# Seven block products instead of eight in one feed-forward layer, and low parts made by adding DMAs

## The chip, the cores and the metric

The kernel runs on one core of one Trainium2 chip. The metric is the device time of one execution in microseconds (us). Two runs of the kernel before took 2017.01 and 2012.07 us, median 2014.54 us. Engines are named as the profile names them: PE (matmuls), PEld (its weight loads), DVE, ACT, POOL, SP (which issues the loads).

## The reference

Two layers of a diffusion backbone. A latent stream and a context stream of 256 tokens each, 1024 features wide, go through the same weights: a gated feed-forward part (FFN), token mixing (differential attention and a Fourier branch, merged by gates), and a second FFN. In the last layer the context stream stops after it has given keys and values. What matters here is the FFN:

```python
def swiglu(u, w_in, w_out):
    a, b = jnp.split(u @ w_in, 2, axis=-1)
    return (jax.nn.silu(a) * b) @ w_out

def ffn_sublayer(x, m, i, g, w_in, w_out):
    u = modulate(rms_norm(x, g), m, i)
    return x + 0.5 * m[:, 3 * i + 2][:, None] * swiglu(u, w_in, w_out)
```

`w_in` is 1024 x 5632: a half for `a` and a half for `b`. All numbers are 32-bit floats.

## The kernel before

**Layout.** Features lie on the 128 partitions, tokens along the free axis: columns 0 to 255 are the latent tokens (LAT), 256 to 511 the context tokens (CTX). `u` is eight chunks of 128 features (KC = 8).

**High and low parts.** A float32 operand is split into `hi`, the value rounded to the matmul's own format, and `lo`, what is left. A product is three matmuls (`mm3`, L373 to L375): hi x hi, hi x lo, lo x hi. In the second FFN of the last layer, with 256 columns, `mm_wide` (L380, L381) puts the two that share `hi` into one matmul of 512 columns.

**The stream of weights.** All weights pass, in order of use, through one stream of 392 blocks of 128 x 1024 numbers (512 KB), eight 128 x 128 tiles each. `Stream.next` asks SP to load blocks some way ahead (`ahead[0]`) and splits blocks a shorter way ahead (`ahead[1]`). The split (`split_pieces`, L192 and L193) is a copy on ACT that rounds (`whi`), and a subtraction raw - hi (`wlo`) on DVE or POOL; the string `lo_on` says which by the block's number ("vvp": two on DVE, one on POOL). Layer 1's FFNs also compute the modulation values, one block of `w_mod` per weight block (`tick`): a dot product on DVE per stream (`junk`, L302), and a small operation on POOL (`mval`, L315 and L317).

**Buffers.** One pool of 46 slots of 4 KB per partition (tag "s") holds raw blocks, hi and lo, `u`, and the FFN's gated values `g` (22 slots of hi and lo side by side). PSUM has 8 banks of 512 numbers.

**The FFN** (`ffn`). 22 pairs j, each of two blocks: `pa` gets 128 features of `a`, `pb` of `b`. Two pairs come first, k by k, each stream by itself, while the norm's results arrive. From the third pair on: eight tiles into `pa`, eight into `pb`, each tile an `mm3` of 512 columns, 48 matmuls a pair; then `gated` (L625 to L627) and `low` (L631). `project_out` multiplies the 22 g's by `w_out`, 66 tiles per three blocks, adds the residual on DVE (L462), and sums squares for the next norm on POOL (`acc`, L424).

**The order of the work** is written out by hand: each engine executes its instructions in the order in which the Python code issues them, and waits on semaphores where the code's reads and writes demand it. A DMA is issued by the engine whose queue it stands in and waits there for its source and its buffer.

## Time and profile before

| | us |
|---|---|
| median of two runs | 2014.54 |
| the profiled execution's own time | 2016.41 |
| its span, first to last instruction | 2014.5 |
| PE busy | 1992.3 |
| DVE busy | 1211.7 |
| ACT busy | 823.0 |
| POOL busy | 735.6 |

Stages by the PE's instructions in the trace, us from the span's start: layer 1's first FFN to 396, mixing and its output to 816, second FFN to 1178; layer 2's first FFN from 1178 (pairs three to five from 1202.6, the sixth pair from 1235.2, the output from 1420.2 to 1541), mixing to 1815, second FFN from 1815 (input from 1828, output from 1942.4), end at 2014.5. The granted clock of the core was 0.997 of full. Where a row of windows is shown, its columns are: the stretch, its length, the busy time and number of instructions (in brackets) of PE, PEld, DVE, ACT and POOL, the granted clock, the share of the 16 DMA engines, GB/s. A matmul's own duration in the trace overlaps the next one's, so its price is taken from the distance of starts, or from a window divided by its count.

### The profile page before, as it was taken

The numbers are of one execution on the slowest core, as the hardware profiler recorded it, in microseconds if no ns is written. First come the engines' busy times: TensorE is split into PE (matmuls) and PEld (weight loads), VectorE is DVE, ScalarE is ACT, GpSimd is POOL, SyncE is SP. The second block draws the span as 40 slices with busy tenths as digits, with TensorE's granted clock in tenths as the row PEclk, the third lists the DMA queues.
The fourth block names the chain that finished last, engine by engine and source line by source line (L and its number), as shares of the span: only waits on it lengthen the run. The fifth ranks groups of instructions, "written<-read, shape, count | busy, mean of one in ns | idle before, by whom it ended". The sixth has DMA issues, their size and how long they took to land.

```text
span 2014.5 us, 26969 instructions
## 1 busy us (share of the span) xinstructions
PE 1992.3 (99%) x10388; PEld 1702.2 (84%) x10388; DVE 1211.7 (60%) x1832; ACT 823.0 (41%) x1335; POOL 735.6 (37%) x492
## 2 busy tenths in 40 slices
PE   8999999999999999999999999999999999999998
PEld 7888888888888888988888898888888889898887
DVE  5877786667777334677777252332324687776652
ACT  3432232256666323523223242222323565666661
POOL 0334455546553013243358410111222454224463
PEclk9999999999999999999999999999999999999999
DMA  9555565413222334455569332222421333555461
GB/s 378 204 169 176 167 210 210 165 58 110 92 85 93 105 105 137 157 172 173 178 212 353 104 131 82 91 74 84 139 91 53 126 128 119 192 172 193 158 203 59
DMA packets 86704, 297.58 MB, mean 148 GB/s; under 512 B 10032, under 2 KB 13232, under 8 KB 86576
## 3 DMA queue, kind: packets, MB, share of 16 engines
q1 hardware_dynamic: 86288, 295.34, 43.7%
q8 instruction: 81, 1.33, 0.3%
q10 hardware_dynamic: 288, 0.52, 0.1%
q14 instruction: 47, 0.39, 0.1%
HBM read 287.44 MB, written 1.05 MB: 143 GB/s over the span
## 4 chain that ended last, share of the span: by engine, by line
PE 93%; DVE 3%; ACT 2%; issue 1%; POOL 1%; DVEq 0%; POOLq 0%; ACTq 0%
PE po L375 7%; PE po L374 7%; PE po L373 7%; PE pa L373 5%; PE pb L375 5%; PE pa L375 5%; PE pb L373 5%; PE pa L374 5%; PE pb L374 5%; PE pg L373 2%; PE pg L375 2%; PE pg L374 2%; PE po L380 2%; PE pb L380 2%; PE pa L380 2%; PE pv L696 1%
## 5 line engine op out<-in xcount | busy, mean ns | idle before, releaser
L193 POOL TENSOR_TENSOR wlo<-wraw,whi 128x1024 fp32r<-128x1024 f32 x139 | 366.0, 2635 | 605.4 <-ACT whi L192 487.1
L192 ACT ACTIVATE whi<-wraw 128x1024 fp32r<-128x1024 f32 x392 | 395.5, 1049 | 74.8 <-PE po L374 34.1
L193 DVE TENSOR_TENSOR wlo<-wraw,whi 128x1024 fp32r<-128x1024 f32 x253 | 350.3, 1394 | 117.9 <-ACT whi L192 116.3
L302 DVE SCALAR_TENSOR_TENSOR junk<-mraw,cond 128x1024 bf16<-128x1024 f32 x224 | 303.1, 1395 | 1.1 <-DMA mraw<-in_w_mod 1.1
L373 PE MATMUL po<-g,whi 128*128 128x512 f32 (+1 forms) x616 | 223.8, 363 | 0.0
L375 PE MATMUL po<-g,wlo 128*128 128x512 f32 (+1 forms) x616 | 223.3, 362 | 0.0
L374 PE MATMUL po<-g,whi 128*128 128x512 f32 (+1 forms) x616 | 223.3, 362 | 0.0
L627 ACT ACTIVATE g<-gv 128x512 fp32r<-128x512 f32 (+1 forms) x92 | 51.7, 562 | 373.6 <-DVE gv L626 344.0
L317 POOL TENSOR_SCALAR mval<-macc,small 128x2 f32<-128x2 f32 (+1 forms) x88 | 122.3, 1394 | 216.2 <-DVE junk L302 216.2
L373 PE MATMUL pa<-u,whi 128*128 128x512 f32 x472 | 183.6, 389 | 0.0
L374 PE MATMUL pa<-u,whi 128*128 128x512 f32 x472 | 183.6, 389 | 0.0
L375 PE MATMUL pa<-u,wlo 128*128 128x512 f32 x472 | 183.6, 389 | 0.0
L373 PE MATMUL pb<-u,whi 128*128 128x512 f32 x472 | 183.6, 389 | 0.0
L374 PE MATMUL pb<-u,whi 128*128 128x512 f32 x472 | 183.6, 389 | 0.0
L375 PE MATMUL pb<-u,wlo 128*128 128x512 f32 x472 | 183.6, 389 | 0.0
L626 DVE TENSOR_TENSOR gv<-silu,pb 128x512 f32<-128x512 f32 x59 | 40.6, 688 | 182.3 <-PE pb L375 181.3
L462 DVE SCALAR_TENSOR_TENSOR x<-po,mval,x 128x256 f32<-128x256 f32 x73 | 32.6, 479 | 194.5 <-PE po L375 194.5
L374 PEld LDWEIGHTS po<-g,whi 128*128 128x128 f32 x616 | 116.3, 189 | 18.3
L373 PEld LDWEIGHTS po<-g,whi 128*128 128x128 f32 x616 | 116.2, 189 | 18.3
L375 PEld LDWEIGHTS po<-g,wlo 128*128 128x128 f32 x616 | 116.2, 189 | 17.9
L424 POOL TENSOR_TENSOR acc<-acc,sq 128x256 f32<-128x256 f32 (+1 forms) x46 | 53.2, 1156 | 191.5 <-ACT sq L413 191.5
L413 ACT ACTIVATE sq<-x 128x256 f32<-128x256 f32 (+1 forms) x48 | 24.7, 516 | 235.3 <-DVE x L462 202.8
(262 smaller groups left out, 4555.2 us busy)
## 6 DMA issues: line engine op xcount, KB each, us to landing
wraw<-in_ffn_in SPq DMA_DIRECT2D x176, 512.0 KB, 4.2
mraw<-in_w_mod SPq DMA_DIRECT2D x128, 512.0 KB, 3.7
wraw<-in_ffn_out SPq DMA_DIRECT2D x88, 512.0 KB, 4.4
wraw<-in_qk SPq DMA_DIRECT2D x32, 512.0 KB, 4.0
wraw<-in_g SPq DMA_DIRECT2D x32, 512.0 KB, 4.4
mfirst<-in_w_mod_first SPq DMA_DIRECT2D x16, 512.0 KB, 10.2
wraw<-in_v SPq DMA_DIRECT2D x16, 512.0 KB, 4.1
wraw<-in_attn SPq DMA_DIRECT2D x16, 512.0 KB, 4.0
```

The source lines that it names most:

```text
L192: nc.scalar.activation(hi[:, c], raw[:, c], AF.Copy)
L193: eng.tensor_tensor(out=lo[:, c], in0=raw[:, c], in1=hi[:, c].bitcast(F32), op=ALU.subtract)
L302: nc.vector.scalar_tensor_tensor(out=tmp.tile([P, D], BF16, tag="t", name="junk"), in0=mod_raw[n], scalar=1.0, in1=cond[s], op0=ALU.mult, ...
L317: eng.tensor_scalar(out=o, in0=v, scalar1=b_mod[:, b:b + 1], scalar2=0.5 if i % 3 == 2 else 1.0, op0=ALU.add, op1=ALU.mult)
L373: nc.tensor.matmul(ps, hi, uh, start=first, stop=False)
L374: nc.tensor.matmul(ps, hi, ul, start=False, stop=False)
L375: nc.tensor.matmul(ps, lo, uh, start=False, stop=last)
L380: nc.tensor.matmul(ps.rearrange("p (a b) -> p a b", a=2), hi, t[:, :, c], start=first, stop=False)
L424: nc.gpsimd.tensor_tensor(out=self.acc[:, c], in0=self.acc[:, c], in1=sq[:, c], op=ALU.add)
L462: nc.vector.scalar_tensor_tensor(out=x[:, m, c], in0=ps[:, c], scalar=mod(l, 3 * i + 2, m, s), in1=x[:, m, c], op0=ALU.mult, op1=ALU.add)
L626: nc.vector.tensor_tensor(out=v[:, c], in0=sl[:, c], in1=pb[:, c], op=ALU.mult)
L627: nc.scalar.activation(g[j][:, 0, c], v[:, c], AF.Copy)
```

## The change

Two things, both told by the code.

**Adding DMAs.** A new helper `split_by_dma`: ACT copies raw to `hi` as before; POOL writes -hi into `lo` (one operand, read from SBUF); and a DMA issued by POOL adds `raw` onto `lo` in SBUF. `lo_on` gets a third letter, "d", for it. It takes the place of "vvp", "vp", "v" and "p" in all FFNs (but for the program's first blocks) and in the second half of each mixing part with its output. Attention's heads and the values before them keep DVE and POOL. 276 whole blocks are split so, 50 stay on DVE and 32 on POOL.

**Seven products.** In layer 2's first FFN, pairs j = 5 to 21 (the sixth to the last) are computed as a 2 x 2 block product in the manner of Strassen and Winograd: rows are a and b, the inner dimension is cut into k = 0..3 and k = 4..7, columns are LAT and CTX. `pack` puts a pair's 16 tiles into two raw blocks in another order: r0 holds a's low half and b's high half, r1 b's low half and a's high half. Four sums of weight blocks per pair (s1, s2, on DVE, in float32) are split as blocks are, and four sums of u (`tq`) are made once. For these sums `modulated` writes u a second time, unrounded (`full`, ACT). Each product is 4 k's x 3 matmuls of 128 x 256: 84 matmuls a pair. The results are joined by ACT and DVE from three banks, `pone`, `ptwo`, `pthree`, some in the middle of their accumulation; the seventh product (a22 with t4) of a pair is issued within the next pair. From j = 6 on the gated values are kept unsplit, two in a slot (`gf`), and all 16 are split after the last pair (`parted` on ACT, `low` on DVE).

```diff
-E_AHEAD, E_LO, E_K = 4, "vp", 2
+E_AHEAD, E_LO, E_K = 4, "d", 2
+SEVEN = {(1, 0): (5, 6)}
...
+def split_by_dma(nc, hi, lo, raw):
+    nc.scalar.activation(hi, raw, AF.Copy)
+    nc.gpsimd.tensor_scalar(out=lo, in0=hi.bitcast(F32), scalar1=-1.0, scalar2=0.0, op0=ALU.mult, op1=ALU.add)
+    nc.gpsimd.dma_start(out=lo, in_=raw, accum_op=ALU.add)
...
+        on = self.lo_on[i % len(self.lo_on)]
+        if on == "d":
+            split_by_dma(nc, hi, lo, raw)
...
+            if keep:
+                q = j % (KC // 2)
+                if q not in full:
+                    full[q] = slot.tile([P, 4, S], F32, tag="s", name="uf")
+                nc.scalar.activation(full[q][:, 2 * (j // (KC // 2)) + s], t[:, c], AF.Identity, bias=mod(l, 3 * i, j, s))
...
-        st.ahead, st.lo_on, st.tick = (6, 2), "vvp", None
+        st.ahead, st.lo_on, st.tick = (6, 2), "d", None
...
+        def sums(q):
+            b = full.pop(q)
+            nc.vector.tensor_tensor(out=b[:, 0], in0=b[:, 0], in1=b[:, 1], op=ALU.subtract)
...
+            tq[q] = [slot.tile([P, 4, S], F32R, tag="s", name="tq") for _ in range(2)]
+            nc.scalar.activation(tq[q][0], b, AF.Copy)
+            nc.vector.tensor_tensor(out=tq[q][1], in0=b, in1=tq[q][0].bitcast(F32), op=ALU.subtract)
...
+            def prepare(j, w):
+                r0, r1 = (st.take(block(j) + n) for n in range(2))
+                h0, l0 = (slot.tile([P, 1024], F32R, tag="s", name=n) for n in ("h0", "l0"))
+                split_by_dma(nc, h0, l0, r0)
...
+                for n in (one, two):
+                    nc.vector.tensor_tensor(out=s1[:, n], in0=r0[:, n], in1=r1[:, one], op=ALU.add)
+                yield
...
+                nc.vector.tensor_tensor(out=s2[:, one], in0=s1[:, two], in1=r0[:, one], op=ALU.add)
+                nc.vector.tensor_tensor(out=s2[:, two], in0=s2[:, one], in1=r1[:, two], op=ALU.add)
+                yield
...
+                split_by_dma(nc, a12[:, one], a12[:, two], r1[:, two])
+                split_by_dma(nc, h1, l1, s1)
+                yield
+                split_by_dma(nc, h2, l2, s2)
+                yield
...
+            for j in range(j0, NF):
...
+                product(p1, w, "a11", b11, True)
+                nc.scalar.activation(v[:, :S], p1[:, :S], AF.Copy)
+                go(j + 1)
+                product(p3, w, "s1", t1, True)
...
+                go(j + 1)
+                if before:
+                    product(ps2[i], ws.pop(i), "a22", t4, False)
+                    result(i, vi, si)
+                product(ps2[j], w, "s2", t2, True)
...
+                product(p1, w, "a12", b21, False)
+                nc.scalar.activation(sl[:, :S], p1[:, :S], AF.Silu)
+                product(p3, w, "s4", b22, False)
...
+                nc.scalar.activation(sl[:, S:], sl[:, S:], AF.Silu)
+                begin(j + 2)
+                go(j + 2)
+                product(ps2[j], w, "s3", t3, False)
...
+                go(j + 2)
+            st.split_to(st.pos + 1)
+            product(ps2[i], ws.pop(i), "a22", t4, False)
+            result(i, vi, si)
+            st.load_to(st.pos + 3)
+            for j in range(held_from, NF):
+                parted(j, v)
+                low(g[j], slice(0, 512), v)
...
-        st.ahead, st.lo_on = ((6, 2), "vvp") if CTX in ss else ((7, 3), "v")
+        st.ahead, st.lo_on = ((6, 2), "d") if CTX in ss else ((7, 3), "d")
```

Two places show how the order of instructions changes. First ACT at the end of layer 2's first FFN input, before: the last two pairs (`silu` of `pa`, the rounded copy `g`), the copies of the weights (`whi`), then the output's table load.

```order
L625 ACTIVATE silu<-pa 128x512
L627 ACTIVATE g_11435<-gv 128x512
L192 ACTIVATE whi<-wraw 128x1024 x2
L625 ACTIVATE silu<-pa 128x512
L627 ACTIVATE g_11504<-gv 128x512
L192 ACTIVATE whi<-wraw 128x1024 x6
L535 ACT_TABLE_LOAD
```

And now, from the last pair's readings of its banks on (`gf` are the kept gated values, sixteen rows like the two shown first):

```order
L799 ACTIVATE gv<-pone 128x256
L802 ACTIVATE gv<-pthree 128x256
L815 ACTIVATE silu<-pone 128x256
L818 ACTIVATE silu<-silu 128x256
L173 ACTIVATE whi<-wraw 128x1024 x2
L766 ACTIVATE g_12737<-gf 128x512
L766 ACTIVATE g_12740<-gf 128x512
...
L766 ACTIVATE g_12782<-gf 128x512
L173 ACTIVATE whi<-wraw 128x1024 x6
L579 ACT_TABLE_LOAD
```

The copies of the output's first two weight blocks moved behind the last pair's silu, and sixteen copies stand between them and those of the third block. Second, POOL in the same FFN, before: POOL's share of the subtractions for the input and for the output's first blocks (`x17`) stands between the sums of squares of layer 1's end and those of this FFN's output.

```order
L424 TENSOR_TENSOR acc<-acc,sq 128x512
L193 TENSOR_TENSOR wlo<-wraw,whi 128x1024
L424 TENSOR_TENSOR acc<-acc,sq 128x512
L424 TENSOR_TENSOR acc<-acc,sq 128x256 x2
L193 TENSOR_TENSOR wlo<-wraw,whi 128x1024 x17
L424 TENSOR_TENSOR acc<-acc,sq 128x512
L193 TENSOR_TENSOR wlo<-wraw,whi 128x1024
```

Now, one pair of the seven products on POOL (`l` and `h` are low and high parts of r0, then of s1 and s2; `a` holds both parts of a12; `s` is a sum in float32):

```order
L174 TENSOR_SCALAR l_10563<-h_10562 128x1024
L175 DMA l_10563<-wraw 128x1024
L174 TENSOR_SCALAR a_10598<-a_10598 128x512
L175 DMA a_10598<-wraw 128x512
L174 TENSOR_SCALAR l_10603<-h_10602 128x1024
L175 DMA l_10603<-s_10567 128x1024
L174 TENSOR_SCALAR l_10622<-h_10621 128x1024
L175 DMA l_10622<-s_10570 128x1024
```

All low parts of the weights now go through POOL's queue here, four passes and four DMAs a pair, where it had one subtraction per three blocks.

More of the change, by code (lines that the diff above doesn't have):

```diff
@@ L73, with ffn_in_order @@
 BEGUN = 3
-E_AHEAD, E_LO, E_K = 4, "vp", 2
+E_AHEAD, E_LO, E_K = 4, "d", 2
 SQ_PARTS = [7, 5]
 STEPWISE = [[0, 3, 3, 1], [4, 2]]
-def ffn_in_order(first):
+SEVEN = {(1, 0): (5, 6)}
+def ffn_in_order(first, seven=NF):
     order = []
@@ L89, in ffn_in_order @@
             order += [(k, j), (k, NF + j)]
-    for j in range(first, NF):
+    for j in range(first, seven):
         order += [(k, j) for k in range(KC)]
         order += [(k, NF + j) for k in range(KC)]
+    low, high = range(KC // 2), range(KC // 2, KC)
+    for j in range(seven, NF):
+        order += [(k, j) for k in low] + [(k, NF + j) for k in high]
+        order += [(k, NF + j) for k in low] + [(k, j) for k in high]
     return order
@@ L171, in __init__ @@
         self.ahead, self.tick, self.lo_on = (6, 2), None, "v"
+        self.whole, self.n_whole = set(), {}
     def load_to(self, b):
@@ L188, in split_pieces @@
         self.hl[i] = (hi, lo)
-        eng = nc.gpsimd if self.lo_on[i % len(self.lo_on)] == "p" else nc.vector
+        on = self.lo_on[i % len(self.lo_on)]
+        if on == "d":
+            split_by_dma(nc, hi, lo, raw)
+            for j in range(n):
+                yield
+            return
+        eng = nc.gpsimd if on == "p" else nc.vector
         for j in range(n):
@@ L194, in split_pieces, with take @@
             yield
+    def take(self, b):
+        self.load_to(b)
+        return self.raw.pop(b)
     def split_to(self, b):
         while self.n_split <= min(b, len(self.blocks) - 1):
+            if self.n_split in self.whole:
+                self.n_split += 1
+                continue
             for _ in self.split_pieces(1):
@@ L356, in tile_kernel @@
     st = Stream(nc, slot, blocks)
+    per_layer = len(blocks) // DEPTH
+    for (l, f), (j, _) in SEVEN.items():
+        b = l * per_layer + (per_layer - 66 if f else 0)
+        st.whole |= set(range(b + 2 * j, b + 2 * NF))
+        st.n_whole[l, f] = b + 2 * j
     def tick():
@@ L433, in total @@
             return rsqrt(ps, D, c, "rinv")
+    full = {}
     def modulated(u, l, i, s, r):
         c = cols([s])
+        keep = i != 1 and (l, i // 2) in SEVEN
         def low(j, t):
@@ L548, in project_out @@
             e.chunk(KC - 2)
-            st.lo_on = "p"
+            st.lo_on = E_LO
             st.split_to(st.pos + E_AHEAD)
@@ L650, in ffn @@
                     later = None
+                if n and k in (3, 7) and full:
+                    sums(min(full))
             before = None
@@ L662, in ffn @@
                 nc.scalar.activation(cond[n], cond[n], AF.Silu)
-        for j in range(first, NF):
+        seven, held_from = SEVEN.get((l, f), (NF, NF))
+        more = sevens(seven, held_from) if seven < NF else iter(())
+        for j in range(first, seven):
             pa, pb = bank("pa"), bank("pb")
-            for ps in (pa, pb):
+            for n, ps in enumerate((pa, pb)):
                 tiles = st.tiles(8)
@@ L671, in ffn @@
                         mm3(ps[:, c], tiles[k], parts(u[k], c), k == 0, k == KC - 1)
+                if full:
+                    sums(min(full))
+                if seven < NF and j >= seven - 2:
+                    some(more, 1 + (j == seven - 1))
             low(*gated(j, pa, pb, c))
+        some(more, 100)
         return project_out(l, i, ss, lambda k: g[k], NF, after, SILU if f else LN_EXP)
@@ L1285, in start @@
             )
-        st.lo_on = "vvp"
+        st.lo_on = "d"
         return ps
@@ L1335 @@
         for f in range(2):
-            dr[f"ffn_in_{l}{f}"] = pack(a["ffn_w_in"][l, f], ffn_in_order(ffn_first(l, f)))
+            dr[f"ffn_in_{l}{f}"] = pack(a["ffn_w_in"][l, f], ffn_in_order(ffn_first(l, f), SEVEN.get((l, f), (NF,))[0]))
             dr[f"ffn_out_{l}{f}"] = pack(a["ffn_w_out"][l, f], FFN_OUT_ORDER)
```

91 lines of the change are left out of this document (added).

## The prediction

> **What bounds the kernel now.** I read the page's busy times and its chain first, then PE's waits, then windows over the stages that the change touches.
>
> ```profile
> PE 1992.3 (99%) x10388; PEld 1702.2 (84%) x10388; DVE 1211.7 (60%) x1832; ACT 823.0 (41%) x1335; POOL 735.6 (37%) x492
> PE 93%; DVE 3%; ACT 2%; issue 1%; POOL 1%; DVEq 0%; POOLq 0%; ACTq 0%
> PE pk L375 <- DVE wlo L193: 1.8, 2, 1.3
> PE pf L373 <- ACT u L1208: 1.6, 1, 1.6
> ```
>
> PE is busy for all but 22 us of the 2014.5 us span, and the longest of its waits in total (the last two rows, from the list of who waited for whom) come to 1.8 and 1.6 us. So making DVE or POOL lighter can give back almost nothing; only fewer or shorter matmuls shorten the kernel, and any new wait of PE lengthens it. What a matmul costs, the windows tell: one over exactly the 17 pairs that are to change, one in a stretch of layer 2 where all matmuls have 256 columns, then layer 2's narrow part (256 tokens), and in it the second FFN's input.
>
> ```profile
> 1235.20:1420.20 185.00, 185.00 (x817) 153.17 (x817) 57.87 (x57) 53.19 (x68) 26.91 (x11) 1.00 0.28 87
> 1752.00:1776.00 24.00, 24.00 (x202) 24.00 (x201) 15.31 (x25) 12.68 (x21) 0.00 (x0) 1.00 0.58 182
> 1736.50:1942.40 205.90, 204.38 (x1391) 188.28 (x1390) 140.15 (x214) 126.20 (x222) 72.01 (x55) 1.00 0.55 179
> 1828.00:1942.40 114.40, 113.63 (x643) 98.05 (x642) 72.50 (x112) 71.81 (x132) 51.42 (x21) 1.00 0.50 165
> ```
>
> The 17 pairs take 185.0 us, 10.88 us each, and PE never stops in them: 185.0 / 816 = 0.2267 us per matmul of 512 columns. The second row gives 24.0 / 201 = 0.1194 us for one of 256 columns, a little more than half, since something fixed comes with each.
>
> **The seven products.** A pair goes from 48 x 0.2267 = 10.88 us to 84 x 0.1194 = 10.03 us: 0.85 us less, 17 pairs, **-14.5 us**. (Break-even is 10.88 / 84 = 0.1295 us; the arithmetic saves an eighth, the fixed part takes back more than a third of that.) What must hide under 10.03 us per pair, by rows of the same operations:
>
> ```profile
> L192 ACT ACTIVATE whi<-wraw 128x1024 fp32r<-128x1024 f32 x392 | 395.5, 1049 | 74.8 <-PE po L374 34.1 <-DVE junk L302 7.9 <-PE po L375 7.6
> L631 DVE TENSOR_TENSOR g<-gv,g 128x512 fp32r<-128x512 f32 x62 | 43.9, 708 | 42.0 <-ACT g L627 41.9
> L441 DVE SCALAR_TENSOR_TENSOR u<-ut,mval,u 128x256 fp32r<-128x256 f32 x72 | 34.5, 479 | 3.4 <-ACT u L447 3.4
> L447 ACT ACTIVATE u<-ut,mval 128x256 fp32r<-128x256 f32 x72 | 35.7, 508 | 35.7 <-DVE ut L446 35.7
> L627 ACT ACTIVATE g<-gv 128x512 fp32r<-128x512 f32 x62 | 39.2, 632 | 338.3 <-DVE gv L626 338.3
> ```
>
> DVE has five passes of 512 and five of 256 columns, 5 x 0.71 + 5 x 0.48 = 5.9 us; ACT three copies of 1024, one of 512 and four small ones, 3 x 1.05 + 0.63 + 4 x 0.51 = 5.8 us. Both fit, and the products of one bank lie two to four products (12 x 0.1194 = 1.4 us each) apart, so that its reader has time. The second write of u (16 x 0.51 = 8.1 us of ACT) and the sums of u fall between 1175 and 1235 us. A window of that stretch,
>
> ```profile
> 1180.00:1190.00 10.00, 10.00 (x84) 9.95 (x83) 7.41 (x11) 5.16 (x8) 2.78 (x2) 1.00 0.63 242
> ```
>
> has PE full, DVE at 7.4 and ACT at 5.2 of 10 us, and DVE loses its subtractions there: nothing, at worst 2 us where the first pairs wait for u.
>
> **The adding DMAs.** Their price is in no row. Per whole block: ACT's copy as before, a POOL pass with one operand, the issue on POOL, the transfer.
>
> ```profile
> L826 POOL TENSOR_SCALAR p<-p,rs 128x512 f32<-128x512 f32 x32 | 22.4, 699 | 26.9 <-DVE rs L825 25.5
> L826 POOL TENSOR_SCALAR p<-p,rs 128x256 f32<-128x256 f32 x16 | 7.5, 483 | 1.1 <-DVE rs L825 0.4
> L193 POOL TENSOR_TENSOR wlo<-wraw,whi 128x1024 fp32r<-128x1024 f32 x139 | 366.0, 2635 | 605.4 <-ACT whi L192 487.1 <-issue 54.2 <-DVE g L631 18.4
> L193 DVE TENSOR_TENSOR wlo<-wraw,whi 128x1024 fp32r<-128x1024 f32 x253 | 350.3, 1394 | 117.9 <-ACT whi L192 116.3 <-DMA wraw<-in_ffn_in 1.3
> L806 SPq DMA_DIRECT2D kh<-kh x32: 461/467/528, 427.7 to 1703.6; - x32
> kh<-kh SPq DMA_DIRECT2D x32, 128.0 KB, 2.2
> wraw<-in_ffn_in SPq DMA_DIRECT2D x176, 512.0 KB, 4.2
> q1 hardware_dynamic: 86288, 295.34, 43.7%
> 357.46 2.24 POOL L317 TENSOR_SCALAR mval<-macc,small 128x2 f32<-128x2 f32 x1 [1.19 <-DVE junk L302]
> 362.05 0.26 POOL L317 TENSOR_SCALAR mval<-macc,small 128x2 f32<-128x2 f32 x1
> ```
>
> *The pass*: 0.48 us for 256 and 0.70 us for 512 columns go on to 1.13 us for 1024, under half of the subtraction's 2.64 us. *The issue*: SP needs 0.46 us for a copy within SBUF (the row of its duration, min/median/max); POOL may need more, so the ends are 0.46 us and, with no row above it, the whole pass that it replaces, 2.64 us. I take 1.0 us, nearer to the row of the same kind of transfer. *The landing*: between 2.2 us (128 KB within SBUF) and 4.2 us (512 KB from memory); I take 3.5 us. *The DMA engines*: 295.34 MB at 43.7% of 2014.5 us is 1.56 us of all 16 engines per 512 KB; one block added costs that if it runs as a copy, twice that if its two inputs pass one after the other. I take once.
>
> What POOL then carries per pair of the seven products: 3 x 1.13 + 0.70 + 4 x 1.0 = 8.1 us of 10.03. In the narrow part a block lasts 16 matmuls, 113.63 / 643 x 16 = 2.83 us, and POOL needs 2.1 us for it. In layer 1's FFNs a block lasts 24 x 0.2267 = 5.4 us; there POOL also has `mval`, which takes 0.26 us by itself and 2.24 us while DVE's dot products run, two rows above: a POOL read waits there for DVE's two-operand passes. Pass, issue, `mval` and a wait of 1.2 us make 4.5 us. All three fit, and DVE's 253 subtractions (1.39 us each) fall to 50, which shortens no path.
>
> The DMA engines are tighter. The narrow part (third window) has them at 0.55 x 205.9 = 113 us; some 70 blocks are added in it, 70 x 1.56 = 109 us: 222 us in 206. The fastest slice of the page,
>
> ```profile
> DMA  9555565413222334455569332222421333555461
> GB/s 378 204 169 176 167 210 210 165 58 110 92 85 93 105 105 137 157 172 173 178 212 353 104 131 82 91 74 84 139 91 53 126 128 119 192 172 193 158 203 59
> ```
>
> moved 378 GB/s, 1.39 us per 512 KB, and by that it is 97 + 97 = 194 us. So it is full to the brim: **+3 us**, from 0 to 16. The Trainium skill, Collectives: The Full Stack, section "The bandwidth ceiling", says that a reducing DMA reads two sources through one ring and so runs at half a copy's rate; the sum by that is the second rival below, and no row here shows an adding DMA.
>
> **The border to the output.** Before, the output's first two blocks are split two blocks ahead; now (second fence on the order of ACT) they are copied after the last pair's silu. Let T be PE's earliest start on the output. The last silu ends about 1.9 us before T (two products follow its bank, 2.9 us, and DVE's subtraction and the silu itself take about 1.0 of these). The first block's hi is ready at T - 0.9, its POOL pass at T + 0.3, its low part lands 3.5 us on, at T + 3.8; PE wants it with its third matmul, at T + 0.4: 3.4 us of waiting. Then 16 copies of 0.632 us hold ACT until T + 10.3; the third block's hi comes at T + 11.4, its low part 1.1 + 3.5 us later, at T + 16.0; PE wants it after 16 x 3 matmuls, at T + 3.4 + 10.9 + 0.4 = T + 14.7: 1.3 us more. **+5 us**, from 0 (a landing of 2.2 us and an earlier copy) to 9 (4.2 us and a dearer issue).
>
> The sum: -14.5 + 3 + 5 = -6.5 us. The profiled execution's own time was 2016.41, its span 2014.5; the median of the runs, 2014.54, happens to equal the span. From the median: **2008 us**. By itself this case runs from 1998 (no new wait at all, 2014.5 - 14.5 = 2000, with the run-to-run spread) to 2016.
>
> **The rivals.** Same to the eye but no gain: low parts arrive a little late again and again. In layer 2's mixing the split runs three blocks of 24 x 0.1194 = 2.9 us ahead, 8.6 us, against 1.05 + 1.13 + 3.5 to 4.2 and a turn in ACT's and POOL's queues. For it: the engines are full there. Against: before, DVE's low parts come out of the same ACT queue without a wait of PE. If each of 25 blocks comes 1 us late: 2008 + 25 = 2033.
>
> Slower, by POOL's issue. POOL is the bound of the seven products from (10.03 - 4.1) / 4 = 1.5 us per issue, of the narrow part from 2.83 - 1.13 = 1.7 us. At 2.64 us: 17 x (4.1 + 4 x 2.64 - 10.03) = 79 and 70 x (1.13 + 2.64 - 2.83) = 66 us, 2008 + 145 = 2153. Against it: SP's 0.46 us. The Trainium skill, DMA: Bandwidth & Descriptors, section "Latency and other measured facts", gives about 1 us for the first byte of a DMA issued by POOL; if that is the issue, POOL does not bind.
>
> Slower, by the DMA engines: each addition costs two passes, 2.78 us at the fastest rate. Then the narrow part needs 113 + 70 x 2.78 = 308 us in 206, +102; a pair of the seven products 2 x 1.39 + 3.5 x 2.78 = 12.5 us, +2.5 x 17 = 42. 2008 - 3 + 144 = 2149. It decides as soon as an addition costs more than (206 - 97) / 70 = 1.56 us in the narrow part. For it: two operands have to be read. Against: both lie in SBUF, and the trace's copies within SBUF land early.
>
> **How the numbers follow.** Forecast 0.60, no gain 0.21, POOL's issue 0.09, two passes 0.09, more than 40 us gained 0.01: nothing in the profile could give that. A difference under 2% (40 us) is about what a measurement of this kernel tells from none. So faster 0.01, same 0.81, slower 0.18. The range takes in the first two cases, 1996 to 2056; the two slow ones lie beyond it.
>
> **What would show it.** Right: windows over the 17 pairs come to about 171 us with PE full; PE's waits name `wlo` at the output's start, some 5 us; POOL's share rises to about 80% in the seven products. Wrong: DMA issues on POOL of over 1.5 us, or landings that grow to 10 us in the narrow part, with PE waiting for low parts all along layer 2; or matmuls of 256 columns at 0.13 us.

## The result, and the profile after

The changed kernel takes **2267.44 us** (2266.04 to 2268.85) against 2014.54: 1.1255 times the kernel before, 95% interval 1.1189 to 1.1322. The forecast of 2008 us and its range are missed by far; the time is 253 us above the kernel before. The page of the changed kernel, busy times, the chain, the DMA engines over the 40 slices and the two queues (q0: the adding DMAs that POOL issues; q1: SP's loads):

```profile
PE 2058.2 (91%) x11000; PEld 1759.4 (78%) x11000; DVE 1078.9 (48%) x1802; ACT 876.3 (39%) x1440; POOL 1089.3 (48%) x1073
PE 31%; issue 30%; POOL 19%; DMA 15%; DVE 2%; ACT 2%; POOLq 0%; SPq 0%; DVEq 0%; ACTq 0%
DMA  9799999633225787999999489997963426999998
q0 software_dynamic: 49536, 175.92, 41.1%
q1 hardware_dynamic: 86288, 295.34, 37.2%
```

PE, which had stopped for 22 us of its span, now stops for 2264.2 - 2058.2 = 206 us, and the chain, 93% PE before, runs over POOL and the DMA engines. These are at 9 or more tenths in 21 of 40 slices. The price that was in no row is now in one: q0 moved 175.92 MB, which is 335.5 blocks of 512 KB, in 0.411 x 2264.2 = 930 us of all 16 engines, **2.77 us for each block added**. A load takes 0.372 x 2264.2 us / 563 = 1.50 us by the same sum. The price is not one of full engines alone: where only six blocks are added beside loads that leave the engines more than half free (experiment 12 below), the same sum gives 2.7 us.

PE's waits, by who was waited for (total, times, longest):

```profile
PE po L411 <- DMA wlo<-wraw: 37.6, 14, 9.6
PE pa L411 <- DMA wlo<-wraw: 17.7, 14, 3.6
PE pthree L742 <- DMA l<-s: 16.4, 8, 4.5
PE pa L417 <- DMA wlo<-wraw: 14.8, 14, 4.5
PE pf L411 <- DMA wlo<-wraw: 13.2, 3, 4.9
PE po L417 <- DMA wlo<-wraw: 12.9, 17, 1.2
```

All the long ones are low parts that have not landed (L411 and L417 are the third matmul, lo x hi), in both layers and in every kind of stage. Windows over layer 1's first FFN (input, output), its second FFN's input, the 17 pairs of the seven products, and layer 2's last part from the output projection through the second FFN's input (columns as before; the last three are the granted clock, the share of the DMA engines, GB/s):

```profile
68.70:293.10 224.40, 212.09 (x914) 171.26 (x913) 131.92 (x194) 61.68 (x80) 127.97 (x113) 0.99 0.92 239
293.10:422.90 129.80, 123.47 (x598) 103.82 (x597) 67.37 (x116) 32.35 (x39) 67.77 (x81) 0.99 1.01 292
895.10:1128.70 233.60, 221.88 (x962) 179.05 (x961) 134.17 (x199) 64.95 (x84) 138.51 (x121) 1.00 0.94 251
1336.40:1564.50 228.10, 189.40 (x1429) 185.22 (x1428) 114.67 (x163) 83.62 (x137) 122.69 (x129) 0.93 0.93 204
1975.60:2175.30 199.70, 162.63 (x935) 137.85 (x933) 59.96 (x119) 96.08 (x166) 110.78 (x136) 0.97 1.04 265
```

The DMA engines are at 0.92 of their time or more in all of them. The 17 pairs took 185.0 us and take 228.1; layer 1's first FFN, of which the prediction priced nothing, goes from 327.7 to 354.2. The terms of one block, POOL's pass (L174), the issue (L175), and the landings:

```profile
L174 POOL TENSOR_SCALAR wlo<-whi 128x1024 fp32r<-128x1024 f32 x276 | 352.4, 1277 | 413.0 <-ACT whi L173 381.0
L175 POOL DMA_DIRECT2D wlo<-wraw x276 | 247.2, 896 | 163.8 <-POOL wlo L174 90.0
wlo<-wraw POOLq DMA_DIRECT2D x276, 512.0 KB, 8.3
wraw<-in_ffn_in SPq DMA_DIRECT2D x176, 512.0 KB, 6.9
```

The pass and the issue cost what was taken for them (1.28 and 0.90 us); the landing takes 8.3 us where 3.5 were taken, and the loads of the same engines went from 4.2 to 6.9.

There is a second effect. One of PE's stops in the seven products, as a timeline of PE, and a window over the 7 us behind it:

```profile
1400.01 0.28 PE L741 MATMUL ptwo<-tq,h 128*128 128x256 f32 x1
1403.97 0.58 PE L742 MATMUL ptwo<-tq,l 128*128 128x256 f32 x1 [3.69 <-DMA l<-s]
1404.35 0.41 PE L740 MATMUL ptwo<-tq,h 128*128 128x256 f32 x1
1404.57 0.41 PE L741 MATMUL ptwo<-tq,h 128*128 128x256 f32 x1
...
1403.00:1410.00 7.00, 6.03 (x30) 6.03 (x31) 0.42 (x1) 0.38 (x1) 2.89 (x3) 0.53 1.08 207
```

PE waits 3.69 us for a low part; then its matmuls of 256 columns come 0.21 us apart in place of 0.12, at a granted clock of 0.53. The clock record of the changed kernel holds 25 such intervals between the start-up and the last 5 us, of 3.4 to 10.2 us, together 126.3 us at half speed, so at most 63 us lost; the kernel before has none there.

Where the 253 us are, by stage, with the runs that tell most (each stage from its first matmul in the trace to the next stage's; "one pass" is experiment 3, "half" 5, "half, ahead" 9, "all, ahead" 10):

```
                         before  after  no seven  one pass   half  half,ahead  all,ahead
L1 first FFN (in+out)     327.7  354.2     354.6     331.5  339.6       329.9      366.2
L1 mixing ... pf          444.1  472.2     468.2     455.7  459.2       443.0      442.7
L1 second FFN (in+out)    338.6  374.0     375.7     342.3  351.4       347.3      361.5
L2 first FFN, pf+input    241.9  295.5     247.9     243.2  246.4       241.1      241.1
L2 first FFN, output      121.0  133.4     121.9     131.1  121.0       121.0      121.0
L2 mixing ... pf          286.8  329.7     326.4     311.4  318.3       292.7      310.9
L2 second FFN (in+out)    186.5  236.6     236.4     191.1  202.3       189.6      241.8
```

### The profile page after: what moved, and what is told of

It reads as the page before. It is cut to its first block, busy times and chain, and to the rows that moved or that the text cites. A ratio compares the mean times of both kernels' runs of the same rounds, so it can differ in the third digit from the quotient of the medians.

```text
span 2264.2 us, 29681 instructions
## 1 busy us (share of the span) xinstructions
PE 2058.2 (91%) x11000; PEld 1759.4 (78%) x11000; DVE 1078.9 (48%) x1802; ACT 876.3 (39%) x1440; POOL 1089.3 (48%) x1073
## 3 DMA queue, kind: packets, MB, share of 16 engines
q0 software_dynamic: 49536, 175.92, 41.1%
## 4 chain that ended last, share of the span: by engine, by line
PE 31%; issue 30%; POOL 19%; DMA 15%; DVE 2%; ACT 2%; POOLq 0%; SPq 0%; DVEq 0%; ACTq 0%
POOL wlo L174 10%; DMA wlo<-wraw 8%; POOL wlo L175 3%; PE po L411 3%; PE po L409 3%; PE po L410 3%; POOL l L174 2%; DMA mraw<-in_w_mod 2%; PE pv L911 1%; PE pg L409 1%; PE pg L410 1%; PE pg L411 1%; PE pv L909 1%; PE pk L411 1%; PE pv L910 1%
## 5 line engine op out<-in xcount | busy, mean ns | idle before, releaser
L174 POOL TENSOR_SCALAR wlo<-whi 128x1024 fp32r<-128x1024 f32 x276 | 352.4, 1277 | 413.0 <-ACT whi L173 381.0
L333 DVE SCALAR_TENSOR_TENSOR junk<-mraw,cond 128x1024 bf16<-128x1024 f32 x224 | 303.4, 1397 | 83.0 <-DMA mraw<-in_w_mod 82.1
L173 ACT ACTIVATE whi<-wraw 128x1024 fp32r<-128x1024 f32 x276 | 279.6, 1048 | 159.8 <-DMA wraw<-in_ffn_out 34.8
L175 POOL DMA_DIRECT2D wlo<-wraw x276 | 247.2, 896 | 163.8 <-POOL wlo L174 90.0
L411 PE MATMUL po<-g,wlo 128*128 128x512 f32 (+1 forms) x616 | 229.4, 372 | 26.4 <-DMA wlo<-wraw 26.3
L411 PEld LDWEIGHTS po<-g,wlo 128*128 128x128 f32 x616 | 118.9, 193 | 49.1 <-DMA wlo<-wraw 30.2
L671 ACT ACTIVATE g<-gv 128x512 fp32r<-128x512 f32 (+1 forms) x75 | 41.0, 546 | 284.4 <-DVE gv L670 261.8
L411 PE MATMUL pa<-u,wlo 128*128 128x512 f32 x336 | 134.1, 399 | 17.9 <-DMA wlo<-wraw 17.7
L216 POOL TENSOR_TENSOR wlo<-wraw,whi 128x1024 fp32r<-128x1024 f32 x32 | 85.7, 2678 | 130.6 <-ACT whi L215 87.1
L411 PE MATMUL pb<-u,wlo 128*128 128x512 f32 x336 | 132.1, 393 | 9.1 <-DMA wlo<-wraw 8.9
L409 PE MATMUL pa<-u,whi 128*128 128x512 f32 x336 | 132.2, 394 | 0.0
L410 PE MATMUL pa<-u,whi 128*128 128x512 f32 x336 | 132.1, 393 | 0.0
L409 PE MATMUL pb<-u,whi 128*128 128x512 f32 x336 | 130.8, 389 | 0.0
L410 PE MATMUL pb<-u,whi 128*128 128x512 f32 x336 | 130.8, 389 | 0.0
L348 POOL TENSOR_SCALAR mval<-macc,small 128x2 f32<-128x2 f32 (+1 forms) x88 | 98.3, 1117 | 56.0 <-DVE junk L333 51.8
```

Of the source, the lines that this page charges most:

```text
L173: nc.scalar.activation(hi, raw, AF.Copy)
L174: nc.gpsimd.tensor_scalar(out=lo, in0=hi.bitcast(F32), scalar1=-1.0, scalar2=0.0, op0=ALU.mult, op1=ALU.add)
L175: nc.gpsimd.dma_start(out=lo, in_=raw, accum_op=ALU.add)
L216: eng.tensor_tensor(out=lo[:, c], in0=raw[:, c], in1=hi[:, c].bitcast(F32), op=ALU.subtract)
L333: nc.vector.scalar_tensor_tensor(out=tmp.tile([P, D], BF16, tag="t", name="junk"), in0=mod_raw[n], scalar=1.0, in1=cond[s], op0=ALU.mult, ...
L348: eng.tensor_scalar(out=o, in0=v, scalar1=b_mod[:, b:b + 1], scalar2=0.5 if i % 3 == 2 else 1.0, op0=ALU.add, op1=ALU.mult)
```

## The experiments

Theory A: an adding DMA holds the 16 DMA engines for 2.77 us per 512 KB, two passes, and the engines are full. Theory B: low parts are late because pass, issue and landing follow one another in POOL's queue, whatever the engines carry. Theory D: the seven products are the cost. Experiments 1, 3, 4, 6, 8 and 10 were run once each.

**1. No seven products, all the adding DMAs.**

```diff
-SEVEN = {(1, 0): (5, 6)}
+SEVEN = {}
```

> The changed kernel with eight products everywhere, so with the adding DMAs alone. Theory A (an adding DMA takes the 16 DMA engines for 2.77 us per 512 KB, twice a load's time, and they are full): the 17 pairs need 2 x 1.49 + 2 x 2.77 = 8.5 us of DMA in 10.9 us and go back from 228 to about 185 us, all other stages stay as slow as in the changed kernel: about 2220 us. Theory B (the low parts come late because POOL's queue handles pass, issue and landing in turn, whatever the DMA engines carry): the pairs ask for 2 low parts in 10.9 us instead of 4 in 10.0, so they recover as well: also about 2220. Theory D (the seven products themselves are what costs): near 2015.

2201.06 us. The whole of the slowdown but 66 us is the adding DMAs': D falls as its main cause. Layer 1, mixing and layer 2's second FFN are as slow as in the changed kernel, and the 17 pairs are back at 185. Of those 66 us the table shows 48 in the FFN's input and 12 in its output.

**2. The seven products, no adding DMA.** Outside the 17 pairs the low parts come as before; inside, r0's from POOL, those of a12, s1 and s2 from DVE.

```diff
+def split_on(eng, nc, hi, lo, raw):
+    nc.scalar.activation(hi, raw, AF.Copy)
+    eng.tensor_tensor(out=lo, in0=raw, in1=hi.bitcast(F32), op=ALU.subtract)
...
-                split_by_dma(nc, h0, l0, r0)
+                split_on(nc.gpsimd, nc, h0, l0, r0)
```

> The seven products kept, all low parts made by subtraction again: outside the 17 pairs as before, inside them r0 on POOL, the others on DVE. Theories A and B: no adding DMA, so the 250 us go, and the seven products bring their 14.5 us less the border to the output: 2000 to 2012 us. Theory D: 2030 or more. DVE then has about 9 of 10 us per pair and may make PE wait: each us of that over 17 pairs is 17 us.

2023.01 us, 1.0042 of before (1.0026 to 1.0059): a miss, no gain at all. The 17 pairs take 181.8 us, 3.2 less than before; pairs 3 to 5 and the output take 4.2 and 7.1 more. PE's longest waits in this run, and the sums s1 on DVE ahead of the first two pairs, the second with the pass of POOL beside it:

```profile
PE po L417 <- POOL wlo L222: 4.5, 1, 4.5
PE pone L746 <- ACT gv L805: 2.5, 1, 2.5
...
1230.29 3.48 DVE L719 TENSOR_TENSOR s<-wraw 128x512 f32<-128x512 f32 x2
1241.29 3.49 DVE L719 TENSOR_TENSOR s<-wraw 128x512 f32<-128x512 f32 x2
1240.95 2.67 POOL L174 TENSOR_TENSOR l<-wraw,h 128x1024 fp32r<-128x1024 f32 x1 [8.33 <-ACT h L173]
```

The first is the third block of the output, split behind 16 copies of g. The second comes from DVE: ACT, for which PE waits, waited for DVE's gating, and that stood behind the two sums, 0.7 us each elsewhere, which took 3.48 and 3.49 us together beside a two-operand pass of POOL.

**3. A plain copy for the addition.** The same transfer without the second source; the low part it leaves is raw itself.

```diff
-    nc.gpsimd.dma_start(out=lo, in_=raw, accum_op=ALU.add)
+    nc.gpsimd.dma_start(out=lo.bitcast(F32), in_=raw)
```

> The changed kernel with the DMA on POOL copying raw over lo instead of adding to it (the low part is then wrong: the subtraction is left out). Same passes, same issues, same waits, same bytes written. Theory A: one pass instead of two, about 1.4 us per block, total DMA time falls from 78% of the span by 20 points, most of the 250 us go: 2010 to 2060 us. Theory B: the queue on POOL and the issue are unchanged, so at least 2200 us.

2076.46 us, 191 less than with the addition. The queue and the landing in this run:

```profile
q0 software_dynamic: 48448, 175.92, 22.2%
wlo<-wraw POOLq DMA_DIRECT2D x276, 512.0 KB, 4.9
L175 POOL DMA_DIRECT2D wlo<-wraw x276 | 161.6, 585 | 111.5 <-POOL wlo L174 107.1
```

0.222 x 2074.7 / 335.5 = 1.37 us per block, half of 2.77. With everything else in place, passes, issues, waits and order, layer 1's FFNs are within 4 us of before. A holds. The copy's issue is also 0.31 us shorter (0.585 against 0.896), so not every one of the 191 us need be the engines'; POOL was under half busy in both. The Trainium skill, Collectives: The Full Stack, section "The bandwidth ceiling", says that a reducing DMA passes two source addresses, hence two reads through one ring, at half a copy's rate; 2.77 against 1.37 agrees. That the second read is the cause no row shows; the ratio is what it would give.

**4. Fewer loads beside the additions.** 6 of the 128 blocks of `w_mod` are loaded, which leaves out most modulation weights.

> The changed kernel with 6 loads of modulation weights instead of 128; the dot products read the same blocks again (the modulation is then wrong: most of its weights are left out). 122 loads of about 1.49 us leave the DMA engines in layer 1's two FFNs. Theory A: these two FFNs, now about 62 us longer than before the change, go back to within 10 us of it, layer 2 stays: about 2215 us. Theory B: POOL's queue and the number of adding DMAs are unchanged: within 10 us of 2267.

2213.84 us: as A had it. Layer 1's first FFN is at 212.9 + 122.9 where the changed kernel has 224.4 + 129.8, the second at 219.7 + 125.7 (233.6 + 140.4): 64 MB less to load give back most of the loss there, with every addition still made. (DVE's waits for these loads, 82.1 us in the changed kernel, go with them, and POOL's for DVE behind them; so the run shows the engines' load as the cause, and not by which wait it reaches PE.) Layer 2, whose loads stay, stays as slow (225.2 in the 17 pairs).

**5. Every second block added by DMA, no seven products.**

```diff
-        st.ahead, st.lo_on, st.tick = (6, 2), "d", None
+        st.ahead, st.lo_on, st.tick = (6, 2), "dv", None
```

> No seven products, and only every second block's low part comes by an adding DMA (the others by DVE's subtraction). Theory A (the 16 DMA engines are full, 2.77 us for an addition): a bound that is fallen below stops to cost. Layer 1's first FFN input has 84 us of loads and 22 x 2.77 = 61 us of additions in 207 us, so it should be back at 207; layer 2's narrow part has 113 + 35 x 2.77 = 210 us in 206 and stays a little over: 2015 to 2035 us in all. Theory B (each low part that comes by DMA is late by itself): half of the additions, half of the loss of the kernel without seven products (187 us), about 2108 us, spread evenly over the stages.

2111.54 us, 1.0488 of before (1.0472 to 1.0504). A's number is missed by over 75 us, B's is met to 4. With 0.75 to 0.81 of the DMA engines' time in use in layer 1's FFNs, and half the additions, half of the loss is still there: so full engines are not all of it. But it isn't spread evenly, as B said: L2's second FFN is back to within 16 us, mixing hardly at all.

**6. The additions without a matmul that reads them.** The kernel before, and each FFN block is also added into one of three spare tiles (the pool has 43 tiles in place of 46).

```diff
+        if self.spare:
+            nc.gpsimd.dma_start(out=self.spare[i % len(self.spare)], in_=raw, accum_op=ALU.add)
```

> The kernel before, every low part by subtraction as there; beside it each FFN block is also added by an adding DMA into one of three spare tiles that nobody reads, so no matmul waits for any of them; the pool of tiles has 43 in place of 46. Theory A (engines full): the transfers alone bring the loss. The FFN stages slow down about as they did with the additions in use, layer 1's input stages to about 220 us each, the narrow part's input from 114 to 140 us or more, and 2120 to 2200 us in all. Theory B (late low parts, not the transfers): nobody waits for these, so 2015 to 2030 us, with only POOL's issue (0.9 us a block) added beside its own subtractions.

2128.17 us. 263 additions of which nothing is read bring 115 us: A's, not B's. PE does not wait for the additions here. The largest part of its stops, 40 of 97 us, is for POOL's own subtractions, since POOL stands in its queue until a spare tile is free again (57.0 us) before it issues the next addition; the loads, too, wait until a raw block has been added. So the loss needs no low part made by a DMA, only transfers that take long; how much of the 115 us the smaller pool has, no run tells. But the stages come out otherwise than expected; windows over layer 1's first FFN, input and output, here and then in the kernel before:

```profile
70.90:280.80 209.90, 206.87 (x913) 171.03 (x911) 157.66 (x215) 60.06 (x79) 106.62 (x85) 1.00 0.97 268
280.80:422.50 141.70, 127.44 (x597) 107.46 (x598) 94.84 (x136) 32.72 (x41) 65.73 (x70) 0.94 0.98 275
```

```profile
67.90:274.60 206.70, 206.70 (x913) 171.16 (x912) 161.74 (x225) 61.46 (x80) 88.33 (x51) 1.00 0.52 173
274.60:395.60 121.00, 121.00 (x597) 102.90 (x597) 85.04 (x127) 32.49 (x39) 63.19 (x43) 1.00 0.57 202
```

The input is hardly longer (206.7 before), the output 21 us (121.0). The sum, 351.6, is near what the engines ask for: by the shares of before and one addition per block, 0.52 x 206.7 + 0.57 x 121 + 66 x 2.77 = 359 us of work, of which a few blocks are added ahead of the stage; the windows' own shares give 0.97 x 209.9 + 0.98 x 141.7 = 342 us. Additions that no matmul waits for are paid late, in the output; where each block is waited for at once, they are paid at once (224.4 + 129.8 in the changed kernel). The whole FFN comes to 351.6 to 354.6 us in experiments 6 and 1 and the changed kernel alike, however the loss is spread over its two stages.

**7. A first mend of the seven products.** Against experiment 2: r0's low part by one adding DMA per pair, and the output's first four blocks split during the last two pairs.

```diff
-                split_on(nc.gpsimd, nc, h0, l0, r0)
+                split_by_dma(nc, h0, l0, r0)
...
+                if j >= NF - 2:
+                    st.lo_on = "d" if j == NF - 2 else "v"
+                    st.split_to(st.pos + 2 * (j - NF + 2))
```

> The seven products, with four edits against the run with the seven products and subtractions (2023 us): the first block of each pair gets its low part by one adding DMA (3 us of loads and 2.8 us of addition in 10 us, and no two-operand pass of POOL beside DVE's sums), and the output's first four blocks are split during the last two pairs in place of after them. Theory D1 (the seven products save their 13 us and lose them at their two ends): the wait of 4.5 us at the output's start with the half clock behind it goes (-7), the one at the first pair as well (-4), 2010 to 2014 us, up to 4 us faster than before. Theory D2 (the small waits inside the 17 pairs and the half clock are its own cost): 2017 to 2022 us, slower than before by 0.2 to 0.4%. Theory A only asks that the adding DMAs find room here: no landing above 8 us.

2024.66 us, 1.0051 (1.0038 to 1.0064): a miss for D1. The output is back at 121.0 us, but the pairs go from 181.8 to 188.2. All of that is lost in the last six of the 17, which take 11.5, 10.7, 13.2, 12.0, 14.6 and 14.9 us; the longest stop of PE is 3.9 us. In these ACT and DVE wait, again and again, for PE or for an adding DMA to be done with something (ACT's copy of a12 waits 2.4 us for PE). The likely reason is a pool that runs out of tiles: an adding DMA holds its raw block longer than a subtraction does, the kept gated values grow in number, and in the last two pairs the output's four blocks come on top. No run shows it by itself.

The pairs before tell more. The second to the eleventh start 10.07 to 10.08 us apart, where they took 10.88 before the change: the forecast's gain of 0.85 us a pair is there, 0.80 of it. In experiment 2 most pairs take 10.3 us. The same 40 us of experiment 2, then of this run:

```profile
1260.00:1300.00 40.00, 39.35 (x322) 38.53 (x321) 38.86 (x51) 19.24 (x32) 10.14 (x4) 1.00 0.34 104
1260.00:1300.00 40.00, 40.00 (x336) 40.00 (x335) 34.59 (x53) 19.31 (x32) 9.77 (x8) 1.00 0.65 168
```

With r0's low part by an adding DMA DVE falls from 38.9 to 34.6 us busy, and PE does 336 matmuls, four pairs, in the place of 322.

**8. What a stop of PE costs.** The kernel before, with eight stops of growing length in layer 2's first FFN input; during the last one PE has 40 other matmuls to do.

> The kernel before, with eight stops of PE put between pairs of layer 2's first FFN input, where PE was full and DMA at 0.28: a chain of 1, 2, 3, 4, 6, 9, 14 and 14 POOL passes of 512 columns (0.7 us each) that PE waits for, the last one with 40 extra matmuls for PE to do meanwhile. Theory H (a stop of PE of about 3 us or more is answered with 3 to 10 us of half clock): no half clock after the stops of 1 to 2.5 us, intervals of half clock after those of 3 us and more, none after the filled one; about 32 us of stops, 9 us of extra matmuls and 4 x 2 to 5 us of half clock, 2065 to 2080 us. Rival (the half clock comes from the load of the DMA engines, not from stops): no half clock at all, 2055 to 2060 us.

2075.18 us, in H's range. The matmul behind the second, third, fourth and seventh stop and behind the filled one (idle time in brackets), and windows right behind the stops:

```profile
1273.24 0.50 PE L645 MATMUL pst<-stall,ones_r 128*128 128x512 f32 x1 [1.82 <-POOL stall L641]
1297.96 0.50 PE L645 MATMUL pst<-stall,ones_r 128*128 128x512 f32 x1 [2.46 <-POOL stall L641]
1325.32 0.50 PE L645 MATMUL pst<-stall,ones_r 128*128 128x512 f32 x1 [3.47 <-POOL stall L641]
1423.82 0.80 PE L645 MATMUL pst<-stall,ones_r 128*128 128x512 f32 x1 [12.16 <-POOL stall L641]
1459.82 0.50 PE L645 MATMUL pst<-stall,ones_r 128*128 128x512 f32 x1 [2.02 <-POOL stall L641]
```

```profile
1273.30:1287.00 13.70, 13.70 (x61) 11.37 (x62) 3.30 (x4) 4.25 (x7) 2.47 (x1) 1.00 0.20 67
1298.00:1303.00 5.00, 5.00 (x15) 3.96 (x16) 3.01 (x2) 1.48 (x2) 2.38 (x1) 0.66 0.01 3
1325.40:1330.40 5.00, 5.00 (x15) 4.00 (x16) 2.08 (x2) 0.42 (x1) 0.00 (x0) 0.66 0.00 0
1423.90:1428.90 5.00, 5.00 (x12) 3.94 (x13) 0.00 (x0) 0.00 (x0) 0.00 (x0) 0.51 0.01 3
1459.90:1464.90 5.00, 5.00 (x22) 4.16 (x23) 0.00 (x0) 0.00 (x0) 2.20 (x1) 1.00 0.00 0
```

After an idle time of 1.82 us the clock stays at 1.00; after 2.46 us and more it is at half for 3 to 6 us of PE's work, whether the stop was 2.5 or 12 us; where PE had matmuls during the same chain and was idle for 2.02 us only, nothing. The DMA engines are nearly idle there, so the rival falls: the half clock follows PE's own stops. In this run a stop of 2.5 us or more so costs its length and about 2 us on top.

**9. Half of the additions, more look-ahead**, and **10. all additions, more look-ahead** (the same numbers with "d" for "dv").

```diff
-E_AHEAD, E_LO, E_K = 4, "dv", 2
+E_AHEAD, E_LO, E_K = 6, "dv", 2
...
-        st.ahead, st.lo_on, st.tick = (6, 2), "dv", None
+        st.ahead, st.lo_on, st.tick = (8, 4), "dv", None
...
-        st.ahead, st.lo_on = ((6, 2), "dv") if CTX in ss else ((7, 3), "dv")
+        st.ahead, st.lo_on = ((8, 4), "dv") if CTX in ss else ((9, 5), "dv")
```

> The kernel with half of the additions and no seven products (2111.5 us), with blocks split 4 ahead in place of 2 (5 for 3 and 6 for 4 in layer 2's narrow part), loads as many further ahead; nothing else. Its demand on the DMA engines is below the time in layer 1 (first input 0.52 x 206.7 + 22 x 2.77 = 168 us of 207). Theory L (below the bound the loss is lateness: landings of 6 to 8 us behind copy, pass and issue do not fit in two blocks): two blocks more of look-ahead take most of the 98 us back, 2015 to 2045 us. Theory A alone (only full engines cost): no change, 2100 us or more, since the engines do the same work.

> The same longer look-ahead with all low parts added by DMA and no seven products (2201 us with the short one). Theory A (full engines, 2.77 us for an addition): the demand stays above the time, layer 1's first input at 0.52 x 206.7 + 44 x 2.77 = 229 us, its second at 0.55 x 217.6 + 122 = 242, the narrow part at 113 + 70 x 2.77 = 307 against 206; those stages keep their length and 2150 to 2190 us remain. Theory L alone (lateness): the longer look-ahead mends it, below 2080 us.

With half of the additions: 2034.07 us, 1.0101 of before (1.0087 to 1.0115). 77 of the 98 us are back with the same transfers; what was left in experiment 5 was lateness, as L had it. With all of them: 2153.57 us, 47 us back and 140 still there, as A had it. PE's longest waits of the first, then of the second run:

```profile
PE po L411 <- DMA wlo<-wraw: 5.9, 4, 2.2
PE pa L417 <- DMA wlo<-wraw: 3.4, 1, 3.4
```

```profile
PE po L411 <- DMA wlo<-wraw: 34.9, 17, 9.0
PE ss L466 <- POOL acc L460: 14.5, 2, 14.0
```

The lengths expected of single stages were wrong again: with the longer look-ahead layer 1's input takes 210.6 us, not 229, and its output 155.6; together 366.2, where the sum of work above is 359 us. 14.0 us of it are the last row: PE waits for a sum of squares that stands in POOL's queue behind modulation values, and these wait for DVE, whose loads of `w_mod` are late. So the full engines reach PE by the loads, too, where the low parts are early enough. The stages that do recover with all additions are layer 1's mixing and layer 2's first FFN, where the engines have room.

**11 and 12. The two ends of the seven products.** Both against experiment 2: the output's first four blocks split behind the last pair, ahead of the copies of g; and, in 12, low parts by adding DMA in pairs 3 to 5, where the engines stand nearly idle.

```diff
-            st.split_to(st.pos + 1)
+            st.split_to(st.pos + 3)
...
+        if (l, f) in SEVEN:
+            st.lo_on = "d"
```

> The run with seven products and subtractions (2023 us), with four in place of two of the output's blocks split right after the last pair, ahead of the 16 copies of g. Theory D1 (the wait of 4.9 us for the third block and the half clock behind it are the border's cost): -7, 2016 us, output stage back from 128.1 to 121 to 122. Rival: the two more copies hold back the copies of g and PE waits for those, 2020 us or more.

> As the run before, and the blocks of pairs 3 to 5 of that FFN get their low parts by adding DMAs (the engines are at 0.12 to 0.20 there), which takes the subtractions of DVE (28.7 of 37 us busy) and POOL out of the stretch in which the sums of u and the first weight sums are made. Theory D1: pairs 3 to 5 go from 36.8 to 33 us and the stop of 2.8 us at the first pair goes, 2010 to 2013 us, no slower than before. Rival (the adding DMAs' low parts are late here too, as in the changed kernel, where this stage took 37.8 us): 2016 us or more.

2017.99 us, 1.0023 (1.0013 to 1.0033), the output at 122.7: the border's price was as expected. Then 2014.34 us, 1.0006 (0.9997 to 1.0015), a little above the expected 2010 to 2013: the pairs come down to 177.3, but pairs 3 to 5 go up to 40.2. In 12, PE's longest wait:

```profile
PE pa L417 <- DMA wlo<-wraw: 4.8, 1, 4.8
```

It is pair 3's second block: its copy on ACT stands behind the gating of the first two pairs, and from its start at 1209.8 us copy, pass, issue and landing take until 1217.0. The half clock behind it lasts 6.8 us.

**13 and 14. Those two stops.** 13 is 12 with the blocks of this FFN split three ahead; 14 also has the low parts of the output's third and fourth block by adding DMA.

```diff
-            st.lo_on = "d"
+            st.ahead, st.lo_on = (7, 3), "d"
```

> As the run with both ends edited (2014.3 us, 1.0006 of before), with the blocks of this FFN split 3 ahead in place of 2, so that ACT's copy for pair 3's second block comes before, not after, the gating of the first two pairs. There that copy came at 1209.8 us, its low part landed after 1217, PE stood 5.2 us and ran 6.8 us at half clock. Theory D1 (the seven products save about 8 us inside, 177.3 against 185, and only stops at the ends take it back): -8, 2005 to 2009 us, faster than before by 0.2 to 0.4%. Theory D2 (the seven products have no gain of their own; DVE, busy for 173 of 189 us, is late elsewhere then): 2012 us or more.

> As the run before, and the output's third and fourth block get their low parts by adding DMAs in place of DVE, which comes to the low parts of g 2.5 us sooner (PE stood 1.7 us there for DVE's low part of g). Theory D1: 1 to 2 us less than the run before, output stage 121 to 121.5 us. Rival: these two low parts land late (half of the loads at that place, 0.5 of the DMA engines), a new stop at the third block, 2 us or more slower.

2014.01 us, 1.0000 (0.9991 to 1.0009), and 2013.85 us, 0.9998 (0.9989 to 1.0007): D2. Pairs 3 to 5 are at 32.7, as before the change, but one more copy of 1 us now stands ahead of the last chunks of u, and PE's longest wait that is new is

```profile
PE pf L415 <- ACT u L492: 2.2, 1, 2.2
```

with an interval of half clock behind it; the first two pairs take 27.8 us in place of 24.3 before the change, and the 17 pairs 180.1 in place of 177.3. The output stays at 122.6 us in 14, where 121 to 121.5 were expected. Windows over the same 178 us of experiments 12 and 13:

```profile
1240.00:1418.00 178.00, 175.89 (x1432) 172.67 (x1431) 162.43 (x214) 83.09 (x136) 37.12 (x15) 1.00 0.29 95
```

```profile
1240.00:1418.00 178.00, 174.09 (x1415) 170.49 (x1413) 163.76 (x215) 81.32 (x134) 37.44 (x16) 1.00 0.29 92
```

DVE (third figure) is at 162 to 164 of 178 us, and PE's waits in these windows are nearly all for it (2.0 of 2.0 us, then 3.1 of 4.0). Experiments 11 to 14 all leave r0's subtraction on POOL, and their pairs take 10.3 us, as in 2. Experiment 7's r0, whose pairs took 10.08, together with the ends of 12 to 14 was not run. The whole FFN, from its first pairs through its output, is at 363.8, 363.2 and 363.2 us in 12, 13 and 14, against 362.9 before.

## Why the prediction was wrong, point by point

**The bound.** Right: PE was the bound, and new waits lengthen the kernel almost one for one (184 us more of idle PE, at most 63 us of half clock, 250 us more of span).

**The step that failed** is the term of the adding DMAs, "one block added costs that if it runs as a copy, twice that if its two inputs pass one after the other. I take once." It is twice: 2.77 us against 1.56 taken, and 1.37 for a copy; and the term of +3 us, worked out for the narrow part alone, stands against some 190 us (187 in experiment 1, which has the additions alone; 191 come back in experiment 3). The argument for once, that both operands lie in SBUF and that copies within SBUF land early, read a latency as if it were the engines' time: a copy of 128 KB that lands in 2.2 us says nothing of how long 16 engines are held by four times as much, and nothing of a second source.

**Where it was added up.** The rival with two passes named this mechanism and gave 2149 us. For the seven products it had 12.5 us a pair, 212 us for the 17: the engines' work was that (0.93 x 228.1 = 212), but the pairs took 228.1, 16 us more, with PE's stops and the half clock. For the narrow part it had 308 us against 206, +102; the same stretch (1900.0 to 2175.3 us) takes 275.3, with the engines at 1.01 of their time: +69. So the one term was too small and the other too large. What the rival left out is layer 1: there the prediction checked POOL, block by block, and never the DMA engines. The row was there to be read: 0.52 to 0.57 of the engines' time in use, and 66 x 2.77 us = 183 us of additions in an FFN of 328. Layer 1 took 90 us more (26 + 28 + 35), most of the 118 by which even that rival fell short; what else it missed lies in layer 2, at the ends of the seven products and in the second FFN's output (17 us).

**Rivals that were taken one at a time.** "Low parts a little late again and again" got 25 us and stood beside the rival with two passes as another case. It is the same case: full engines lengthen the landings from the 4.6 us (median) that the six additions of experiment 12 take to 8.3, and a look-ahead of two or three blocks that fits the first does not fit the second. Experiments 5 and 9 put 77 us on it with half of the additions alone. The landing's range of 2.2 to 4.2 us came from transfers of a kernel whose engines were half idle. The term "+3" for the DMA engines and the one for the landing should have been one question: how long is the queue.

**POOL's issue.** The rival falls: 0.896 us, near the 1.0 taken, far from the 1.5 at which POOL binds. The 1 us that the Trainium skill gives (DMA: Bandwidth & Descriptors, "Latency and other measured facts") is of that size, though the page says it of the first byte. The pass, 1.28 us against 1.13, was a little dearer.

**The border.** Right in place and order, wrong in size: PE stops for 9.6 us, not 3.4, since the low part lands later (10.2 us behind its issue, the median of the three there, where 3.5 were taken), and half clock follows; the output takes 12.4 us more, not 5.

**The seven products.** The price of the matmuls was right: the middle pairs of experiment 7 run at 10.08 us where 10.03 were forecast (by the distance of starts a matmul of 256 columns takes 0.1200 us). But the most that any run gave inside all 17 pairs is 7.7 us of the 14.5 (185.0 to 177.3), and across the FFN nothing is left. "Nothing, at worst 2 us where the first pairs wait for u" was the wrong step here: the second write of u, the sums and the first weight sums fall into 30 us, and the stop went from DVE to POOL's landing to ACT as each was mended. With r0's subtraction on POOL the middle pairs are held by DVE, at 97% there; without it they are not. A version without the losses at both ends was not found, so whether the gain can be kept stays open.

**Not foreseen at all**: the half clock.

## What to carry to other kernels

Price a new DMA by the time that it holds the engines, not by when one lands: multiply it by the number of transfers, add the share in use in *every* stage it enters, and compare with the stage's time; near the full, landings grow too, and a look-ahead that was enough is not. Work moved off engines that were not the bound (DVE at 60%) gains nothing, and can fill the resource that was half empty. A gain of a few per cent inside a loop can be lost at its two ends, so cost the first and the last pass of a new schedule as carefully as the middle.

## What the runs showed of the hardware

An adding DMA within SBUF holds the engines for 2.77 us per 512 KB (2.7 to 3.0 in the other runs), a copy of the same tiles for 1.37, and its issue takes POOL 0.896 us, a copy's 0.585.

PE's granted clock falls to half behind its own stops: not after 1.82 us of idle time, always after 2.46 us and more in experiment 8. There the half clock begins 3.5 to 4.6 us after the stop does, and ends 3.6 to 5.7 us after PE is at work again. The bound is not sharp: in experiment 13 half clock follows a stop of 2.2 us, and in the changed kernel a stop of 3.3 us, at 1507 us, has none behind it (granted clock 1.00 from 1505 to 1520 us). The Trainium skill, TensorE: Matmul & The Clock Gate, section "HAM oscillation — how this bites in real kernels", gives idle gaps of more than about 3.4 us as the condition; here a gap of 2.46 us was enough, and the measurement decides.

A two-operand pass of POOL holds up a two-operand pass of DVE beside it. In experiment 2 the groups of DVE's sums, of which the first runs beside POOL's subtraction of r0 in each pair and the second mostly after it (count, busy time, mean ns):

```profile
L722 DVE TENSOR_TENSOR s<-s,wraw 128x512 f32<-128x512 f32 x17 | 42.2, 2479 | 0.1
L723 DVE TENSOR_TENSOR s<-s,wraw 128x512 f32<-128x512 f32 x17 | 13.9, 815 | 0.6
```

The same operation on the same shape takes 2.48 and 0.82 us. A subtraction given to POOL costs DVE 1.7 us there, more than the 1.39 us that one of its own took in the kernel before. That POOL is slowed as well, no row shows.
